# A list scheduler in the kernel for ScalarE's and VectorE's order in the FFNs, and two transposed blocks to a PSUM bank

## The chip, the cores and the metric

The kernel runs on one core of a Trainium2 chip. Its time is the device time of one execution in microseconds; the time before is the median of three runs, 957.65 us (956.59 to 960.48). The engines that matter are TensorE (PE in the profile; PEld is its weight load), VectorE (DVE), ScalarE (ACT), GpSimd (POOL), and SyncE (SP), which only starts DMAs here.

## What is computed

A trunk of two layers over 256 tokens of width 1024, in float32. Each layer is a half-step SwiGLU FFN, a mixer of a pooling group and a gated recurrence, and a second FFN, each followed by a layer norm. The change concerns the FFNs, four in all, with an inner width of 2816:

```python
D_MODEL, SEQ, DEPTH = 1024, 256, 2
D_FF = ((8 * D_MODEL // 3 + 127) // 128) * 128

def swiglu(x, w_gate, w_up, w_down):
    return (jax.nn.silu(x @ w_gate) * (x @ w_up)) @ w_down

for l in range(DEPTH):
    x = layer_norm(ALPHA * x + 0.5 * swiglu(x, ffn1_gate[l], ffn1_up[l], ffn1_down[l]), ln_g[l, 0], ln_b[l, 0])
    ...
    x = layer_norm(ALPHA * x + mix, ln_g[l, 1], ln_b[l, 1])
    x = layer_norm(ALPHA * x + 0.5 * swiglu(x, ffn2_gate[l], ffn2_up[l], ffn2_down[l]), ln_g[l, 2], ln_b[l, 2])
```

## The kernel before

**Numbers.** Every float32 operand is split into a high half in float32r and the remainder (`halves`, L114: ScalarE casts, VectorE subtracts). A product is three matmuls, high by high, high by low, low by high (`mm3`, L109 to 112). A weight arrives as a raw tile of 128 x 1024 (512 KB) by a DMA on SP's queue (L142) into one of five raw slots; ScalarE casts it to `wh` (gate and up weights) or `dh` (down weights) at L115, VectorE makes `wl` or `dl` at L116. Eight such pairs are held for gate and up, six for down.

**Groups.** The inner width is cut into eleven groups g of 256. `G` (one half of the tokens, hf) and `GT` (both halves, result transposed) compute a group's gate and up; `D` multiplies the gated group by its down weights into PSUM accumulators (`acc`). A `GT` has 32 matmuls of 128 x 512 with the high weights (`gu<-xt,wh`, the high pass) and 32 of 128 x 256 with the low ones (`gu<-xt,wl`, the low pass), all at L536. It holds all four PSUM banks of the pool `psg` (tiles named `gu`). Its result comes out with the inner dimension on the partitions, as D wants it; ScalarE and VectorE copy, add, gate and halve it (`gate_turned`, L553 to 563).

**Pairs.** In the three FFNs that are not the first, the groups 4 and 5, and 7 and 8, are computed as two pairs by a scheme of seven products instead of eight. Step `A` has 36 matmuls, step `B` 48; VectorE makes the sums of raw weights that they need (L225, L230 to 233). After B, ScalarE copies one accumulator (`u`, L491), VectorE makes four sums of 128 x 512 (L492 to 495), and then three times a silu (ScalarE, L505) and a product (VectorE, L506) give blocks of gated values in tiles named `cb`: u, p5 and v; a fourth, c11, was already made after A. These have the tokens on the partitions, so each of the four must be transposed for D: `T` (L648 to 657) does two transposes of 128 x 128 at L651 into a PSUM bank of its own, ScalarE casts the high half `hth`, VectorE subtracts `htl`, and the bank is free again.

**Order.** TensorE's order is the order of the code. Each FFN's steps stand in a list (`order`, L384 to 409); behind a pair come D of the two halves of the group before the pair and then GT of the group after it. Work that waits for another engine, such as T, is put into a queue, `Later` (L47 to 73), with a number of slots; a slot passes with each `mm3`, or with its length in GT. The slots of a pair's four T are 2, 6, 7 and 7 (L498 to 500). GT first empties that queue (`later.wait(lambda: not self.pending)`), since it needs all four banks. The order on ScalarE and VectorE is made by the tile scheduler when the program is built; the code steers it with priorities (AHEAD for gates, sums, products and halves of transposes, BEHIND for weight loads). Each engine then runs its instructions in that fixed order.

## Time and profile before

| what | us |
|---|---|
| median of three runs (lowest, highest) | 957.65 (956.59, 960.48) |
| the profiled execution | 958.14 |
| its span | 956.4 |
| TensorE, a `mm3` matmul of 128 x 512, mean | 0.39 |
| VectorE, a weight's low half of 128 x 1024 (`wl`, 255 of them), mean | 1.22 |
| ScalarE, a weight's high half (`wh`, 255 of them), mean | 1.05 |
| VectorE, 128 x 256 product or sum | 0.42 |
| DMA of a gate and up weight, issue to landing, median | 4.5 |

The durations of rows overlap: matmuls start 0.23 us apart though each is shown with 0.39, and VectorE's instructions also start before the one before them has ended. Where it matters, the text counts from start to start. The granted clock of TensorE is 0.998 of the full one in the profiled execution. In the rows of the timeline, a bracket at the end gives the idle time before the instruction and what ended it.

### The profile page before, as it was taken

The page shows a single profiled execution, that of the slowest core. Times are in us where ns is not written, and L with a number is a line of the kernel's source. Part 1 is how long each engine was busy: PE and PEld are TensorE (multiplying, and loading weights), DVE is VectorE, ACT ScalarE, POOL GpSimd, SP SyncE. Part 2 cuts the span into 40 slices and gives each one's busy share as a digit, 9 for nine tenths or more (in the row PEclk, how much of TensorE's full clock was granted, in tenths as well). Part 3 has the DMA queues.
Part 4 walks back from the last instruction along what each step waited for, and adds up shares of the span by engine and source line. Part 5 has one row for each costly group of instructions (what it writes and reads, how often), then busy time and mean ns, then how long its engine had stood idle before and what let it go on. Part 6 is the DMA issues. An engine that isn't in the chain of part 4 may idle for free.

```text
span 956.4 us, 13068 instructions
## 1 busy us (share of the span) xinstructions
PE 931.6 (97%) x4695; PEld 782.9 (82%) x4695; DVE 770.5 (81%) x1233; ACT 553.0 (58%) x840; POOL 22.7 (2%) x38
## 2 busy tenths in 40 slices
PE   9999999999999999989999989999999999999996
PEld 7888888888988887868888868788898888878685
DVE  6885755779879889897877799967899797899945
ACT  7775544377546656575455466753975466565630
POOL 0000000000010000000000000000000000000000
PEclk9999999999999999999999999999999999999999
DMA  8887853333725758878337578783417357588811
GB/s 301 314 297 265 286 205 112 141 116 105 243 89 192 277 180 285 276 273 287 122 135 261 169 251 295 271 290 100 136 63 264 130 187 260 190 277 280 271 78 45
DMA packets 57665, 198.92 MB, mean 208 GB/s; under 512 B 6784, under 2 KB 7040, under 8 KB 57600
## 3 DMA queue, kind: packets, MB, share of 16 engines
q1 hardware_dynamic: 57264, 197.43, 60.0%
q8 instruction: 37, 0.61, 0.3%
q0 software_dynamic: 192, 0.53, 0.2%
q14 instruction: 28, 0.23, 0.1%
q10 hardware_dynamic: 144, 0.13, 0.0%
HBM read 197.01 MB, written 1.05 MB: 207 GB/s over the span
## 4 chain that ended last, share of the span: by engine, by line
PE 76%; DVE 10%; DMA 9%; issue 3%; ACT 2%; SPq 0%; DVEq 0%; ACTq 0%
PE gu L111 24%; PE acc L111 22%; PE gu L536 22%; DMA raw<-in_gu 5%; DMA raw<-in_dn 3%; DVE wl L116 3%; PE gu L1006 2%; DVE dl L116 2%; PE acc L932 1%; PE gu L194 1%; PE acc L611 1%; ACT wh L115 1%; DVE htl L116 1%; PE acc L878 1%; ACT dh L115 1%
## 5 line engine op out<-in xcount | busy, mean ns | idle before, releaser
L115 ACT CAST wh<-raw 128x1024 fp32r<-128x1024 f32 x255 | 266.8, 1054 | 169.4 <-DMA raw<-in_gu 51.0
L116 DVE TENSOR_TENSOR wl<-raw,wh 128x1024 fp32r<-128x1024 f32 x255 | 306.6, 1220 | 28.0 <-ACT wh L115 25.3
L111 PE MATMUL gu<-wh,xt 128*128 128x512 f32 x720 | 239.2, 393 | 0.0
L111 PEld LDWEIGHTS gu<-wh,xt 128*128 128x128 f32 x720 | 135.1, 188 | 28.2 <-DVE xt L116 0.5
L536 PE MATMUL gu<-xt,wh 128*128 128x512 f32 x600 | 143.0, 392 | 3.6 <-DVE htl L116 2.9
L111 PE MATMUL gu<-wl,xt 128*128 128x512 f32 x360 | 140.5, 390 | 0.0
L111 PE MATMUL acc<-dh,hth 128*128 128x512 f32 x354 | 140.4, 397 | 0.0
L111 PE MATMUL acc<-dh,htl 128*128 128x512 f32 x354 | 138.1, 390 | 0.0
L111 PE MATMUL acc<-dl,hth 128*128 128x512 f32 x354 | 137.6, 389 | 0.0
L536 PEld LDWEIGHTS gu<-xt,wh 128*128 128x128 f32 x600 | 112.1, 188 | 31.1 <-DVE htl L116 7.2
L116 DVE TENSOR_TENSOR dl<-raw,dh 128x1024 fp32r<-128x1024 f32 x88 | 106.2, 1219 | 23.5 <-ACT dh L115 23.1
L115 ACT CAST dh<-raw 128x1024 fp32r<-128x1024 f32 x88 | 91.8, 1050 | 40.4 <-DMA raw<-in_dn 34.3
L111 PEld LDWEIGHTS gu<-wl,xt 128*128 128x128 f32 x360 | 67.7, 188 | 13.6
L111 PEld LDWEIGHTS acc<-dh,htl 128*128 128x128 f32 x354 | 66.4, 188 | 14.1
L111 PEld LDWEIGHTS acc<-dl,hth 128*128 128x128 f32 x354 | 66.6, 188 | 12.2
L111 PEld LDWEIGHTS acc<-dh,hth 128*128 128x128 f32 x354 | 66.6, 188 | 11.9
L536 PEld LDWEIGHTS gu<-xt,wl 128*128 128x128 f32 x600 | 74.8, 192 | 1.4
L536 PE MATMUL gu<-xt,wl 128*128 128x256 f32 x600 | 75.7, 283 | 0.0
L559 DVE TENSOR_TENSOR sil<-gu,sil 128x256 f32<-128x256 f32 x42 | 17.6, 419 | 40.4 <-ACT sil L558 40.3
L111 PE MATMUL gu<-wl,Sh 128*128 128x512 f32 x96 | 37.7, 392 | 0.8 <-DVE wl L116 0.8
L111 PE MATMUL gu<-wh,Sh 128*128 128x512 f32 x96 | 37.5, 391 | 0.0
L111 PE MATMUL gu<-wh,Sl 128*128 128x512 f32 x96 | 37.4, 390 | 0.0
(211 smaller groups left out, 1110.0 us busy)
## 6 DMA issues: line engine op xcount, KB each, us to landing
raw<-in_gu SPq DMA_DIRECT2D x208, 512.0 KB, 4.5
raw<-in_dn SPq DMA_DIRECT2D x88, 512.0 KB, 5.3
raw<-in_win SPq DMA_DIRECT2D x40, 512.0 KB, 4.4
raw<-in_wout SPq DMA_DIRECT2D x16, 512.0 KB, 4.5
lng<-in_ln_g SPq DMA_DIRECT2D x6, 512.0 KB, 6.4
lnb<-in_ln_b SPq DMA_DIRECT2D x6, 512.0 KB, 7.2
x<-in_first SPq DMA_DIRECT2D x4, 384.0 KB, 4.3
raw<-in_first SPq DMA_DIRECT2D x4, 384.0 KB, 6.3
```

The source lines that it names most:

```text
L111: nc.tensor.matmul(ps, a, b, start=start and n == 0, stop=stop and n == 2, skip_group_check=more)
L115: first = nc.scalar.copy(dst_h, src)
L116: return first, nc.vector.tensor_tensor(dst_l, src, dst_h.bitcast(F32), ALU.subtract)
L194: nc.tensor.transpose(pt[:, k - a, :], self.nat[:, k * P:(k + 1) * P], ident)
L536: nc.tensor.matmul(ps[i][part][:, 2 * S - w:], weight.parts[lo][:, c:c + P], x[:, 0:w], start=kt == 0 and not lo, stop=kt == KT - 1 and lo ...
L559: nc.vector.tensor_tensor(dst, p[:, 0:S], dst, ALU.add)
L611: nc.tensor.matmul(ps[i][part][:, 2 * S - w:], ws[k // 2].parts[lo][:, c:c + P], xs[:, 0:w], start=k == 0 and not lo, stop=k == KT - 1 and ...
L878: nc.tensor.matmul(pe[:, a:], lf[hf][c][:, h * P:(h + 1) * P], cumM[:, c, a:], start=True, stop=True)
L932: nc.tensor.matmul(dst[:, 2 * j:2 * j + 2, :], side[:, j, :], E[:, 2 * j:2 * j + 2, t0:t0 + dst.shape[2]], start=True, stop=True)
L1006: nc.tensor.matmul(ps[i // 2][:, i % 2, :], w, x, start=kt == 0 and n == 0 and i % 2 == 0, stop=kt == KT - 1 and n == 2 and i % 2 == 1)
```

## The change

Inside the FFNs, the order on ScalarE and VectorE is no longer made by the tile scheduler. Code in the kernel keeps a list of outstanding instructions (`Work`), each with a cost (a fixed part and a part for each column), what it must come after, and a rank; `Desk` holds a model time for each engine, advances with each matmul that is emitted, and emits the instruction that can start earliest by that model, lowest rank first. Weight casts and subtractions have ranks in the order of the weights; gates, sums, products and halves have rank 0. Each emitted instruction is pinned behind the one before it on its engine, without a semaphore. DMA starts follow a model of five raw slots with 1.65 us between loads and 4.6 us to land.

A pair's four blocks are transposed in two groups of two blocks, each group of four transposes into one PSUM bank; a group is emitted only when the model says that its products are done and a bank is free. GT behind a pair does its high pass block by block, 16 matmuls into the first two banks and then 16 into the other two, and asks for the last two only then. It no longer empties the whole queue first. No instruction is added or removed on any engine.

```diff
+LAG = 2
+FIXED, EACH = {"A": 0.155, "V": 0.153, "P": 0.95}, {"A": 0.000875, "V": 0.001042, "P": 0.0}
+HOP, DRAIN, LOAD, ARRIVE = 0.1, 0.25, 1.65, 4.6
+NORM, SUMS, GRACE = 6.5, 8, 0.25
+MM, MMN, FLIP = 0.2275, 0.1195, 0.11
...
 class Later:
...
     def run(self, until):
+        while True:
+            items = [q for q in self.queue if q[0] <= until and (q[3] is None or q[3]())]
+            if not items:
                 return
+            self.take(items)
...
+class Work:
...
+        self.cost = FIXED[engine] + width * EACH[engine]
...
+    def begin(self):
+        return max([self.at] + [a.done + HOP * (a.engine != self.engine) for a in self.after])
...
+class Desk:
...
+    def step(self, until=None):
+        best = None
+        for e in FIXED:
+            ready = [w for w in self.waiting if w.engine == e and w.ready()]
+            if not ready:
+                continue
+            at = max(self.free[e], min(w.begin() for w in ready))
+            w = min((w for w in ready if w.begin() <= at + GRACE * (w.rank < 1)), key=lambda w: w.rank)
+            at = max(at, w.begin())
+            if best is None or at < best[0]:
+                best = at, w
+        if best is None or until is not None and best[0] > until:
+            return False
+        at, w = best
+        self.waiting.remove(w)
+        ins = w.fn()
+        if w.engine != "P":
+            if w.engine in self.last:
+                self.pin(ins.ins, self.last[w.engine])
+            self.last[w.engine] = ins.ins.name
+        self.clock = w.done = self.free[w.engine] = at + w.cost
...
+    order = lambda ins, name: tc.add_manual_dep(
+        ins, name, mybir.DependencyInfo(mybir.DependencyClass.NoSync, mybir.DependencyReason.DATA), reason="in turn")
+    desk = Desk(order)
...
         def B(self, g):
-            later.wait(lambda: not self.pending)
...
-            for slots, n, hf, c in ((2, g, rows[0], self.c11), (6, g + 1, rows[0], u), (7, g + 1, rows[1], self.p5),
-                                    (7, g, rows[1], v)):
-                self.turn(slots, n, hf, c[:, GW:])
...
+            parts = [(g, rows[0], *self.c11), (g + 1, rows[0], u, self.product(u, two)),
+                     (g + 1, rows[1], p5, self.product(p5, three)), (g, rows[1], v, self.product(v, four))]
+            for some in (parts[:2], parts[2:]):
+                self.turn(LAG, *[(n, hf, c[:, GW:], work) for n, hf, c, work in some])
...
+        def turn(self, slots, *parts):
+            self.pending.update(part[:2] for part in parts)
+            later(slots, lambda: self.T(*parts), lambda: desk.over(*[part[3] for part in parts]) and Bank.free())
...
         def GT(self, g):
-            later.wait(lambda: not self.pending)
-            ps = [[psg.tile([P, 2 * S], F32, name="gu") for _ in range(2)] for _ in range(2)]
+            later.wait(lambda: self.turned(g - 1) or g - 1 in self.twice or all((g - 1, hf) in self.ht for hf in range(2)))
+            banks = [[Bank(), Bank()], None]
...
-                blocks = [[0], [1]] if lo or g == 2 and not self.first else [[0, 1]]
+                blocks = [[0], [1]] if lo or self.split(g) else [[0, 1]]
...
+        def split(self, g):
+            return not self.first and (g == 2 or g - 1 in self.twice)
...
+        def T(self, *parts):
+            desk.need(*[part[3] for part in parts])
+            bank, works = Bank(), []
+            for n, (g, hf, hn, _) in enumerate(parts):
+                pt = bank.tile[:, n * 2 * P:(n + 1) * 2 * P].rearrange("p (k t) -> p k t", k=2)
+                src = hn() if callable(hn) else hn
+                for i in range(2):
+                    nc.tensor.transpose(pt[:, i, :], src[:, i * P:(i + 1) * P], ident)
+                    desk.spend(FLIP)
+                works += self.turn_out(g, hf, pt)
+            bank.read(*works)
```

Tile names and lines of the changed kernel: `mm3` is at L234, a weight's halves at L303 and L306, the sums of raw weights at L454, GT at L807, T's transposes at L946 and its halves at L956 and L960, the copy of u at L758, the sums behind B at L756, silu and product at L772 and L773.

**TensorE** behind the first pair of the FFN that follows Mixer 0, from the 18th matmul of D behind B on. Before, T of c11 stands after the sixth matmul of D, u's after the 18th, and p5's and v's after the 21st of 24:

```order
L111 MATMUL acc<-dh,htl 128x512
L651 MATMUL gu<-ident,cb 128x128 x2
L111 MATMUL acc<-dh,hth 128x512
L111 MATMUL acc<-dl,hth 128x512
L111 MATMUL acc<-dh,htl 128x512
L651 MATMUL gu<-ident,cb 128x128 x4
L111 MATMUL acc<-dh,hth 128x512
L111 MATMUL acc<-dl,hth 128x512
L111 MATMUL acc<-dh,htl 128x512
L536 MATMUL gu<-xt,wh 128x512 x32
L536 MATMUL gu<-xt,wl 128x256 x32
```

After, from the 23rd matmul of D behind B on:

```order
L234 MATMUL acc<-dl,hth 128x512
L234 MATMUL acc<-dh,htl 128x512
L946 MATMUL gu<-ident,cb 128x128 x4
L807 MATMUL gu<-xt,wh 128x512 x3
L946 MATMUL gu<-ident,cb 128x128 x4
L807 MATMUL gu<-xt,wh 128x512 x29
L807 MATMUL gu<-xt,wl 128x256 x32
```

All 24 matmuls of D now come ahead of the first transposes; the second group stands behind three matmuls of GT. The same holds at all six pairs. In the FFNs behind the mixers, except the last, the transposes of group 10's first half also come three D matmuls later.

**VectorE** at the end of the same step B; L492 to L495 are the four sums, L506 the products, `htl` the transposes' low halves. Before:

```order
L116 TENSOR_TENSOR dl<-raw,dh 128x1024
L116 TENSOR_TENSOR wl<-raw,wh 128x1024 x4
L492 TENSOR_TENSOR cb<-cb,gu 128x512
L116 TENSOR_TENSOR wl<-raw,wh 128x1024
L493 TENSOR_TENSOR cb<-cb,gu 128x512
L494 TENSOR_TENSOR cb<-cb 128x512
L116 TENSOR_TENSOR htl<-gu,hth 128x256
L495 TENSOR_TENSOR cb<-cb,gu 128x512
L506 TENSOR_TENSOR cb<-cb 128x256 x2
L116 TENSOR_TENSOR dl<-raw,dh 128x1024
L506 TENSOR_TENSOR cb<-cb 128x256
L116 TENSOR_TENSOR htl<-gu,hth 128x256
```

After, from the last sum of raw weights on:

```order
L454 TENSOR_TENSOR raw<-raw 128x512
L306 TENSOR_TENSOR dl<-raw,dh 128x1024 x2
L306 TENSOR_TENSOR wl<-raw,wh 128x1024 x4
L756 TENSOR_TENSOR cb<-cb,gu 128x512 x2
L756 TENSOR_TENSOR cb<-cb 128x512
L756 TENSOR_TENSOR cb<-cb,gu 128x512
L773 TENSOR_TENSOR cb<-cb 128x256 x3
L306 TENSOR_TENSOR wl<-raw,wh 128x1024
L960 TENSOR_TENSOR htl<-gu,hth 128x256 x4
```

The four sums and three products stand together, behind two `dl` and four `wl`, and the four `htl` follow in one piece. Before, a `wl`, an `htl` and a `dl` stood among them.

**ScalarE** at the same place; L491 is the copy of u, L505 a silu, `hth` the transposes' high halves. Before:

```order
L115 CAST wh<-raw 128x1024 x4
L491 COPY cb<-gu 128x512
L115 CAST wh<-raw 128x1024
L115 CAST dh<-raw 128x1024
L115 CAST hth<-gu 128x256
L115 CAST dh<-raw 128x1024
L505 ACTIVATE cb<-cb 128x256 x2
L115 CAST dh<-raw 128x1024
L505 ACTIVATE cb<-cb 128x256
L115 CAST hth<-gu 128x256
L115 CAST dh<-raw 128x1024
L115 CAST hth<-gu 128x256 x2
```

After, L758 is the copy, L772 the silu:

```order
L303 CAST wh<-raw 128x1024 x4
L758 COPY cb<-gu 128x512
L303 CAST wh<-raw 128x1024
L303 CAST dh<-raw 128x1024
L772 ACTIVATE cb<-cb 128x256 x3
L303 CAST dh<-raw 128x1024
L956 CAST hth<-gu 128x256 x4
L303 CAST dh<-raw 128x1024 x2
```

The three silu stand together behind one `wh` and one `dh`, where the first two stood behind a `wh`, two `dh` and an `hth`, and the third behind one `dh` more. The four `hth` follow with one `dh` between.

On SP the order of the DMAs differs only in the loads of the norm's two rows, one group of weights earlier in three FFNs; on POOL one `pow` stands earlier at the end of the first FFN.

## Prediction

> **What bounds the kernel now.** I read the page first, then busy time by stretches, then what TensorE waits for, then its timeline behind the pairs.

> ```profile
> span 956.4 us, 13068 instructions
> PE 931.6 (97%) x4695; PEld 782.9 (82%) x4695; DVE 770.5 (81%) x1233; ACT 553.0 (58%) x840; POOL 22.7 (2%) x38
> ```

> TensorE (PE) is busy 97% of the span, VectorE (DVE) 81%, ScalarE (ACT) 58%. So the end is set by TensorE's own work, 931.6 us, plus the 24.8 us in which it stands still. The change adds no work to TensorE and takes none away. It can only win in those 24.8 us (more by start times, below).

> The stretches show where they lie. The columns are length, then PE, PEld, DVE, ACT and POOL with counts, the granted clock, DMA share and GB/s. The first is in the first FFN, which has no pairs; the six others run from the end of each pair's step B to the start of the low pass of the GT behind it.

> ```profile
> 8.70:165.00 156.30, 156.29 (x835) 135.43 (x836) 109.82 (x161) 98.23 (x158) 0.00 (x0) 1.00 0.73 255
> 369.12:385.81 16.69, 14.47 (x65) 11.08 (x64) 15.23 (x21) 10.35 (x16) 0.00 (x0) 1.00 0.83 283
> 419.68:437.32 17.64, 15.10 (x65) 10.92 (x64) 15.98 (x21) 12.54 (x18) 0.00 (x0) 1.00 0.83 294
> 558.16:575.51 17.35, 14.40 (x66) 11.08 (x64) 15.20 (x21) 10.35 (x16) 0.00 (x0) 1.00 0.77 276
> 609.38:625.93 16.55, 14.89 (x66) 10.99 (x64) 15.50 (x21) 11.30 (x18) 0.00 (x0) 1.00 0.79 270
> 843.20:859.68 16.48, 14.48 (x65) 11.08 (x64) 15.19 (x21) 10.61 (x18) 0.00 (x0) 1.00 0.80 273
> 893.55:910.99 17.44, 15.13 (x65) 10.93 (x64) 15.96 (x21) 12.04 (x18) 0.00 (x0) 1.00 0.80 277
> ```

> The first FFN has nothing to win: 156.29 of 156.30 us. The six stretches behind the pairs last 102.15 us together (16.69 + 17.64 + 17.35 + 16.55 + 16.48 + 17.44), each with the same work. The view of waits names the causes (total us, times, longest):

> ```profile
> PE gu L651 <- DVE cb L506: 8.9, 9, 2.3
> PE gu L536 <- DVE htl L116: 2.9, 3, 1.0
> PE gu L111 <- DVE wl L116: 0.8, 1, 0.8
> ```

> L651 is a transpose T, waiting for VectorE's product (L506). L536 is GT, waiting for the subtraction that gives a transpose's PSUM bank back. Both stand only in the six stretches; the 0.8 us at L111 is a weight's low half in a step B.

> **The change, term by term.** First the price of a stretch without stalls: 24 D matmuls, GT's high pass of 32 matmuls, eight transposes.

> ```profile
> 791.09 11.11 PE gu L536 x64
> 802.20 5.46 PE acc L111 x24
> 17.19 7.46 PE L536 MATMUL gu<-xt,wh 128*128 128x512 f32 x32
> 24.49 1.72 PE L536 MATMUL gu<-xt,wl 128*128 128x256 f32 x13
> 471.70 1.04 PE L194 MATMUL gu<-ident,x 128*128 128x128 f32 x8
> 472.49 0.48 PE L111 MATMUL acc<-dh,hth 128*128 128x512 f32 x1
> 472.81 0.40 PE L111 MATMUL acc<-dl,hth 128*128 128x512 f32 x1
> ```

> The 24 D take 5.46 us (0.2275 each); the high pass takes 24.49 - 17.19 = 7.30 us; eight transposes take 472.49 - 471.70 = 0.79 us, and the next matmul starts 0.32 instead of 0.23 us after the one before it, so 0.88 in all. Together 13.64 us, six times 81.8. The ceiling of the gain is 102.15 - 81.8 = 20.3 us. The first pair of the FFN behind Mixer 0 shows how the excess is made up:

> ```profile
> 373.23 0.39 PE L111 MATMUL acc<-dh,htl 128*128 128x512 f32 x1
> 375.18 0.44 PE L651 MATMUL gu<-ident,cb 128*128 128x128 f32 x2 [1.56 <-DVE cb L506]
> ...
> 377.07 0.41 PE L651 MATMUL gu<-ident,cb 128*128 128x128 f32 x2 [0.53 <-DVE cb L506]
> ...
> 378.02 7.96 PE L536 MATMUL gu<-xt,wh 128*128 128x512 f32 x32
> 385.81 3.99 PE L536 MATMUL gu<-xt,wl 128*128 128x256 f32 x32
> ```

> Start to start, u's transposes come 375.18 - 373.23 - 0.23 = 1.72 us late, v's by at least the 0.53 of its row, and the high pass takes 7.79 instead of 7.30 because its third and fourth bank come back late. The second pair of each FFN pays the last kind as a whole wait:

> ```profile
> 428.31 1.00 PE L536 MATMUL gu<-xt,wh 128*128 128x512 f32 x2
> 430.28 7.21 PE L536 MATMUL gu<-xt,wh 128*128 128x512 f32 x30 [0.97 <-DVE htl L116]
> ```

> 430.28 - 428.31 for two matmuls of 0.23 is 1.5 us of standing still. What a stretch keeps is at least the 13.64 us above; if the switches to and from the transposes make these twice as dear, 14.52. I take 14.0, nearer to the lower end because D and GT run without loss in the rows of the chain. **18.1 us** go: 102.15 less six times 14.0 (ends: 20.3 and 15.0).

> Now what the change does there. The transposes move behind all 24 D, as two groups of four: the first (c11 and u) is due 24 matmuls or 5.46 us after B's end, where c11 was due after 6 and u after 18; the second (p5 and v) after four transposes of 0.11 and three matmuls of GT more, 5.46 + 0.44 + 0.68 = 6.6 us. Both must find VectorE's products done. Its four sums and three products now stand together behind four `wl`, with no `wl`, `dl` or `htl` between, which is the second half of the gain. I place them for this pair with its own rows, in which a row of three gives VectorE's start spacing.

> ```profile
> 365.20 3.50 DVE L116 TENSOR_TENSOR wl<-raw,wh 128x1024 fp32r<-128x1024 f32 x3
> 369.07 1.22 DVE L116 TENSOR_TENSOR wl<-raw,wh 128x1024 fp32r<-128x1024 f32 x1 [0.37 <-ACT wh L115]
> 372.45 0.68 DVE L493 TENSOR_TENSOR cb<-cb,gu 128x512 f32<-128x512 f32 x1
> 373.04 0.68 DVE L494 TENSOR_TENSOR cb<-cb 128x512 f32<-128x512 f32 x1
> 376.51 0.42 DVE L506 TENSOR_TENSOR cb<-cb 128x256 f32<-128x256 f32 x1
> 370.22 1.05 ACT L115 CAST wh<-raw 128x1024 fp32r<-128x1024 f32 x1 [0.70 <-DMA raw<-in_gu]
> 372.01 1.05 ACT L115 CAST dh<-raw 128x1024 fp32r<-128x1024 f32 x1 [0.74 <-DMA raw<-in_dn]
> 374.25 0.71 ACT L505 ACTIVATE cb<-cb 128x256 f32<-128x256 f32 x2
> ```

> The fourth `wl` is over at 370.3. Four sums 0.6 apart (373.04 - 372.45) end by 372.8. ScalarE's three silu stand behind one `wh` and one `dh` cast, which waits for its DMA until 372.01 and ends at 373.06; at 0.35 each they run to 374.1. With 0.42 for a product, u is over at 373.8 and v at 374.5, not at 376.93 as before. Needed: 369.12 + 5.46 = 374.6 and 375.7. So both groups find their operands, 0.8 and 1.2 us ahead. In the second pairs VectorE is further ahead of TensorE (row 414.55 below), and the lead should be larger. The four `hth` and `htl` follow at once, and GT's second pair of banks is asked for 13 matmuls (3.0 us) after the second group, some 1.5 us after the last `htl`. The stall is gone unless one of these leads is.

> What comes late next is the last `wl` of step B in the second pair, since TensorE gets there three microseconds earlier and VectorE has hardly any idle time between the pairs:

> ```profile
> 376.93:417.18 40.25, 39.98 (x190) 33.31 (x191) 37.34 (x49) 23.24 (x32) 0.00 (x0) 1.00 0.79 262
> 414.55 2.35 DVE L116 TENSOR_TENSOR wl<-raw,wh 128x1024 fp32r<-128x1024 f32 x2
> 417.18 0.39 PE L111 MATMUL gu<-wl,Sh 128*128 128x512 f32 x1
> ```

> The first of these two `wl` ends at 415.8 and is used at 417.18, a lead of 1.4 us. TensorE comes 16.69 - 13.64 = 3.05 us earlier here, and 3.71 and 2.84 in the two other FFNs. If VectorE's stream stayed where it is and the lead is 1.4 in all three, 3.05 + 3.71 + 2.84 - 4.2 = 5.4 us would be given back; if it moves forward with the products, by 376.93 - 374.5 = 2.4 us, nothing here and little there. I take **1.0**, nearer to nothing because the products move and the 40.25 - 37.34 = 2.9 us of idle time give way.

> [...]

> **Small terms.** The transposes of G10's first half come behind nine D instead of six in two FFNs, so their halves are three matmuls (0.7 us) later for D10: zero to 0.7 each, I take 0.25. The subtractions of the transposed activations at the start of the three pair FFNs stand behind one `dl` more: zero to 0.5 each, a tenth taken. Together 0.6. The 0.8 us wait at L111 is left in. ScalarE's and VectorE's instruction counts are the same, the DMA order on SP differs by two loads of the norm's rows one group earlier, and POOL's pow in the first FFN is hidden in 156 us without a wait.

> **Sum** against the profiled execution, 958.14 us (a span of 956.4 and 1.74 around it): 958.14 - 18.1 + 1.0 + 0.6 = 941.6. That execution lies 0.5 above the median of the runs shown, 957.65, so I forecast **941.0 us**.

> **The rivals.**
> *VectorE becomes the bound between the pairs.* For it: 37.34 of 40.25 us busy. Against: the products come forward. All 5.4 given back in place of 1.0 is 945; with half as much again at the weights of A and GT, which the same stream makes, 948.

> *Only the place on TensorE helps, the products stay as late as now.* u's transposes now start at 375.18, 0.6 us after the first group is due, and v's product ends at 376.93, 1.2 after the second. Some 1.2 us in each first pair, half in each second one, where one wait fewer stands: 3.6 + 1.8 = 5.4, so 946 to 947.

> *The pin doesn't bring what its table says, or every microsecond moves to the next weight wait.* Then the time stays at 955 to 959. For it: DMA is at 0.77 to 0.83 in these stretches. Against: no wait of TensorE for a weight is in the list but 0.8 us.

> *Slower.* ScalarE runs in a fixed order, so the three silu now stand behind a `dh` cast whose DMA was already late (0.74 us of waiting in the row above).

> ```profile
> raw<-in_dn SPq DMA_DIRECT2D x88, 512.0 KB, 5.3
> ```

> If that load lands L later, TensorE stands at the first transpose for L - 0.8, with nothing else to run. It decides from L = 3.8 (0.8 + 18.1/6); with a whole landing of 5.3 us the six pairs cost 27 us, and the time is 958.1 - 18.1 + 27 - 0.5 = 966. Against: the loads keep their order and come from the same slots. [...]

> **How the numbers follow.** Forecast (937 to 945) 0.68; VectorE bound 0.10; products late 0.10; no change 0.06; slower 0.06. The floor is 958.1 less 20.3, less the 0.8 at L111, less 0.5: 936.5, which I round to 937, as the whole ceiling is unlikely. The upper end takes in both middle rivals with 2 us of room. A measurement of this kernel tells about 0.5% (4.8 us) from no change; the three first cases lie beyond it, less a remainder: faster 0.87, same 0.07, slower 0.06.

> **What would show it.** In the changed profile the waits for `cb` should fall from 8.9 us to under 1.5, those for `htl` from 2.9 to under 0.5, and each of the six stretches should last 13.7 to 14.3 us. VectorE's busy time should stay at 770 us within 2, its share rising as the span shrinks. A new wait for `wl` in the second step B, above 1 us, would show the first rival; transposes that still wait for `cb` the second; a silu long after its sum, behind a `dh` cast, the fourth. The forecast is wrong if the loads land later than now, since every lead worked out here is about one microsecond.

## The result, and the profile after

| | before | after |
|---|---|---|
| median of the runs, us (lowest, highest) | 957.12 (955.40, 960.48) | 983.40 (982.28, 984.08) |
| ratio to before, 95% interval | | 1.0269 [1.0239, 1.0299] |
| the profiled execution, us | 958.14 | 983.54 |
| its span, us | 956.4 | 981.8 |
| granted TensorE clock | 0.998 | 0.978 |
| six stretches from B's end to GT's low pass, us | 102.15 | 82.0 |
| six steps B (48 matmuls each), us | 67.1 | 99.4 |
| first FFN, GT1's start to the D after GT2, us | 27.70 | 41.30 |

The change makes the kernel 2.7% slower where 1.7% faster was forecast. The three last rows of the table hold nearly all of it: -20.1 + 32.3 + 13.6 = +25.8 us, against +25.4 in the span. The page of the changed kernel (busy time, then two rows of its 40 slices in tenths):

```profile
span 981.8 us, 13056 instructions
PE 942.6 (96%) x4695; PEld 792.5 (81%) x4695; DVE 777.5 (79%) x1233; ACT 552.3 (56%) x840; POOL 22.0 (2%) x38
...
PE   9599999999999999989999999899999999999896
...
PEclk9799999999999999989999999999999999999898
```

TensorE has the same 4695 matmuls and is busy 11 us longer: some of them ran slower (48 start 0.43 us apart in place of 0.23). The second slice is a hole, and the granted clock dips there and again near the pairs. The forecast's gain is there all the same. These are the six stretches from the end of a pair's step B to the start of GT's low pass in the changed kernel, with the columns of the prediction:

```profile
386.19:399.90 13.71, 13.71 (x65) 11.35 (x64) 12.07 (x18) 8.72 (x15) 0.00 (x0) 1.00 0.63 221
441.04:454.68 13.64, 13.64 (x66) 11.29 (x64) 10.71 (x16) 8.04 (x14) 0.00 (x0) 1.00 0.54 191
578.47:592.14 13.67, 13.67 (x66) 11.29 (x65) 11.58 (x18) 8.61 (x14) 0.00 (x0) 1.00 0.64 215
632.72:646.38 13.66, 13.66 (x66) 11.29 (x64) 11.96 (x18) 8.83 (x14) 0.00 (x0) 1.00 0.58 207
868.27:881.91 13.64, 13.64 (x65) 11.29 (x64) 11.86 (x18) 8.23 (x13) 0.00 (x0) 1.00 0.59 205
922.72:936.41 13.69, 13.69 (x66) 11.29 (x65) 11.54 (x18) 8.50 (x14) 0.00 (x0) 1.00 0.62 197
```

They sum to 82.0 us, at the floor of 81.8. What TensorE waits for now is elsewhere. Its view of waits (total us, times, longest) in the changed kernel has no row for a transpose and none for `htl`:

```profile
PE gu L807 <- DVE sil L836: 11.2, 2, 10.3
PE gu L234 <- DVE wl L306: 10.2, 9, 1.8
PE gu L234 <- ACT wh L303: 8.2, 6, 2.0
```

The first row is GT2 in the first FFN, waiting for the gates of GT1. The two others are weights' halves in the six steps B. The steps B as windows, first of the changed kernel, then two of before:

```profile
370.90:386.19 15.29, 13.01 (x49) 10.02 (x48) 13.76 (x15) 9.55 (x11) 0.00 (x0) 0.89 0.75 260
422.86:441.04 18.18, 14.41 (x49) 10.55 (x48) 17.48 (x20) 11.15 (x12) 0.00 (x0) 0.81 0.79 274
563.32:578.47 15.15, 12.86 (x50) 9.99 (x49) 14.26 (x15) 9.71 (x12) 0.00 (x0) 0.89 0.81 262
615.09:632.72 17.63, 13.60 (x50) 9.99 (x49) 16.23 (x18) 10.61 (x12) 0.00 (x0) 0.90 0.80 267
852.91:868.27 15.36, 13.07 (x50) 10.07 (x48) 14.07 (x15) 9.58 (x11) 0.00 (x0) 0.89 0.78 262
904.87:922.72 17.85, 14.10 (x50) 10.29 (x48) 16.65 (x18) 10.91 (x12) 0.00 (x0) 0.81 0.78 267
```

```profile
408.77:419.68 10.91, 10.91 (x49) 9.01 (x48) 9.66 (x11) 7.61 (x8) 0.00 (x0) 1.00 0.77 259
545.86:558.16 12.30, 11.53 (x50) 8.93 (x49) 10.31 (x12) 7.06 (x8) 0.00 (x0) 1.00 0.75 237
```

Before, five of six lasted 10.9 to 11.2 us, and 545.86 was the one that waited for a `wl`. Now all six are long, the second pair's more than the first's. VectorE is not the limit: it idles in four of the rows for over a microsecond, and the weights still come late.

**Where the first FFN stops.** GT1's low pass is over at 27.4 us; ScalarE copies its accumulators (L838) and VectorE adds to the copies (L836), which frees the banks for GT2. Before, the first copy ran at 26.54, still inside the low pass:

```profile
26.54 0.37 ACT L558 COPY sil<-gu 128x256 f32<-128x256 f32 x1 [2.17 <-PE gu L536]
```

ScalarE's timeline in the changed kernel:

```profile
38.46 1.04 ACT L303 CAST dh<-raw 128x1024 fp32r<-128x1024 f32 x1 [1.79 <-DMA raw<-in_dn]
40.62 1.04 ACT L303 CAST dh<-raw 128x1024 fp32r<-128x1024 f32 x1 [1.12 <-DMA raw<-in_dn]
41.58 0.37 ACT L838 COPY sil<-gu 128x256 f32<-128x256 f32 x1
```

Two `dh` casts stand pinned ahead of the copies and wait for their DMAs, the last until 40.62. Six casts of earlier loads (at L243, 27.91 to 36.67) also run ahead of the copies here. The copy itself waits for nothing. TensorE, meanwhile:

```profile
43.32 1.22 PE L807 MATMUL gu<-xt,xh 128*128 128x512 f32 x2 [10.29 <-DVE sil L836]
```

The table put the casts there by its own clock: its model of loads starts empty when the first FFN opens, though 15 loads have been issued by then. In its clock these two land 6.25 and 7.9 us after the opening and GT1's gates come at 9.44 (numbers that the list scheduler gives while the kernel is built); on the chip the loads land 22 and 24 us after it.

**What is late in step B.** ScalarE (ACT) and VectorE (DVE) ahead of the first pair's step A, changed kernel; step A starts at 359.95:

```profile
355.43 0.37 ACT L838 COPY sil<-gu 128x256 f32<-128x256 f32 x1 [6.79 <-PE gu L807]
355.84 0.42 DVE L836 TENSOR_TENSOR sil<-gu,sil 128x256 f32<-128x256 f32 x1 [4.55 <-ACT sil L838]
361.88 2.14 DVE L454 TENSOR_TENSOR raw<-raw 128x512 f32<-128x512 f32 x3
```

The same place before, where step A starts at 347.01:

```profile
336.53 0.69 DVE L230 TENSOR_TENSOR raw<-raw 128x512 f32<-128x512 f32 x1 [0.17 <-DMA raw<-in_gu]
...
342.49 0.37 ACT L558 COPY sil<-gu 128x256 f32<-128x256 f32 x1 [0.75 <-PE gu L536]
```

Before, the sums of raw weights for step B begin 10.5 us ahead of step A, ahead of GT's gates (L558). Now ScalarE stands 6.79 us and VectorE 4.55 us with nothing to do, because the pinned order has GT's gates next; the sums of step B's first weights (L454) come behind all of the gates, 1.9 us after step A has started. By the trace their loads had landed 9.0, 7.7 and 5.3 us ahead of step A. By the table's clock they land 0.4 to 3.7 us behind its start, so it saw no reason to put the sums in front. B's first `wl` ends 5.20 us after A's start (2.04 before), its last 22.03 (19.42). A raw slot comes free with its `wl`, so the next loads start later too: the first load of a `dh` behind these starts 12.7 us after A's start (9.7 before).

### The profile page after: what moved, and what is told of

Read it like the earlier page. It is cut to its first block, busy times and chain, and to the rows that moved or that the text cites. A ratio compares the mean times of both kernels' runs of the same rounds, so it can differ in the third digit from the quotient of the medians.

```text
span 981.8 us, 13056 instructions
## 1 busy us (share of the span) xinstructions
PE 942.6 (96%) x4695; PEld 792.5 (81%) x4695; DVE 777.5 (79%) x1233; ACT 552.3 (56%) x840; POOL 22.0 (2%) x38
## 3 DMA queue, kind: packets, MB, share of 16 engines
HBM read 197.01 MB, written 1.05 MB: 202 GB/s over the span
## 5 line engine op out<-in xcount | busy, mean ns | idle before, releaser
L303 ACT CAST wh<-raw 128x1024 fp32r<-128x1024 f32 x191 | 197.4, 1050 | 107.9 <-DVE raw L454 35.4
L306 DVE TENSOR_TENSOR wl<-raw,wh 128x1024 fp32r<-128x1024 f32 x191 | 229.1, 1221 | 30.4 <-ACT wh L303 30.0
L234 PE MATMUL gu<-wh,xt 128*128 128x512 f32 x720 | 240.4, 394 | 0.0
L234 PEld LDWEIGHTS gu<-wh,xt 128*128 128x128 f32 x720 | 136.0, 189 | 29.0 <-DVE xt L248 0.9
L807 PE MATMUL gu<-xt,wh 128*128 128x512 f32 x600 | 142.0, 392 | 0.0
L234 PE MATMUL gu<-wl,xt 128*128 128x512 f32 x360 | 141.0, 392 | 0.0
L234 PE MATMUL acc<-dh,hth 128*128 128x512 f32 x354 | 138.9, 393 | 0.0
L234 PE MATMUL acc<-dh,htl 128*128 128x512 f32 x354 | 138.1, 390 | 0.0
L234 PE MATMUL acc<-dl,hth 128*128 128x512 f32 x354 | 137.6, 389 | 0.0
L807 PEld LDWEIGHTS gu<-xt,wh 128*128 128x128 f32 x600 | 111.7, 188 | 23.0
L306 DVE TENSOR_TENSOR dl<-raw,dh 128x1024 fp32r<-128x1024 f32 x80 | 94.8, 1220 | 16.9 <-ACT dh L303 16.5
L303 ACT CAST dh<-raw 128x1024 fp32r<-128x1024 f32 x80 | 83.1, 1052 | 34.2 <-DMA raw<-in_dn 32.2
L243 ACT CAST wh<-raw 128x1024 fp32r<-128x1024 f32 x64 | 67.3, 1058 | 22.8 <-PE acc L234 8.0
L234 PEld LDWEIGHTS gu<-wl,xt 128*128 128x128 f32 x360 | 68.2, 189 | 13.9
L234 PEld LDWEIGHTS acc<-dh,htl 128*128 128x128 f32 x354 | 66.5, 188 | 14.4 <-DVE htl L960 0.3
L234 PEld LDWEIGHTS acc<-dh,hth 128*128 128x128 f32 x354 | 66.8, 189 | 13.0 <-ACT hth L956 0.4
L234 PEld LDWEIGHTS acc<-dl,hth 128*128 128x128 f32 x354 | 66.6, 188 | 12.9
L807 PEld LDWEIGHTS gu<-xt,wl 128*128 128x128 f32 x600 | 74.8, 192 | 1.4
L807 PE MATMUL gu<-xt,wl 128*128 128x256 f32 x600 | 75.7, 283 | 0.0
L454 DVE TENSOR_TENSOR raw<-raw 128x512 f32<-128x512 f32 x96 | 63.9, 687 | 1.7 <-DMA raw<-in_gu 0.9
L836 DVE TENSOR_TENSOR sil<-gu,sil 128x256 f32<-128x256 f32 x42 | 17.7, 421 | 54.9 <-ACT sil L838 54.9
## 6 DMA issues: line engine op xcount, KB each, us to landing
raw<-in_gu SPq DMA_DIRECT2D x208, 512.0 KB, 4.5
raw<-in_dn SPq DMA_DIRECT2D x88, 512.0 KB, 4.9
raw<-in_win SPq DMA_DIRECT2D x40, 512.0 KB, 4.3
raw<-in_wout SPq DMA_DIRECT2D x16, 512.0 KB, 4.4
lng<-in_ln_g SPq DMA_DIRECT2D x6, 512.0 KB, 6.8
lnb<-in_ln_b SPq DMA_DIRECT2D x6, 512.0 KB, 7.3
```

The lines of the kernel that those rows point to most:

```text
L234: nc.tensor.matmul(ps, a, b, start=start and n == 0, stop=stop and n == 2, skip_group_check=more)
L243: first = nc.scalar.copy(dst_h, src)
L303: return nc.scalar.copy(self.parts[0], self.raw)
L306: second = desk("V", ET, lambda: nc.vector.tensor_tensor(self.parts[1], self.raw, self.parts[0].bitcast(F32), ALU.subtract), [first], rank ...
L454: return desk("V", 512, lambda: nc.vector.tensor_tensor(dst, a, b, op), after, rank, None, **kw)
L807: nc.tensor.matmul(banks[i][part].tile[:, 2 * S - w:], weight.parts[lo][:, c:c + P], x[:, 0:w], start=kt == 0 and not lo, stop=kt == KT - ...
```

## The experiments

Two theories at the start. **The table's order**: both losses come from an order fixed by a model that has the loads late (step B) or early (first FFN). **The place**: TensorE reaches each step B three microseconds sooner, and weights would be late in any order. All sums below are counted from the starts of matmuls in the timeline of one profiled execution each (that of e1_backlog, 973.28 us, lies 4.2 over its median); the ratio is to the kernel before on the same chip.

| kernel | median us | ratio, 95% | six stretches | first B, three | second B, three | first FFN |
|---|---|---|---|---|---|---|
| before | 957.12 | 1 | 102.15 | 34.4 | 32.7 | 27.70 |
| after | 983.40 | 1.0269 [1.0239, 1.0299] | 82.0 | 45.8 | 53.7 | 41.30 |
| e1_backlog | 969.06 | 1.0125 [1.0108, 1.0142] | 83.0 | 46.7 | 54.8 | 27.70 |
| e5_nopin | 946.49 | 0.9890 [0.9875, 0.9905] | 89.5 | 33.0 | 34.6 | 27.68 |
| e6_pin_act | 982.82 | 1.0272 [1.0252, 1.0293] | 83.1 | 40.7 | 55.7 | 42.46 |
| e4_peonly | 988.17 | 1.0335 [1.0317, 1.0353] | 132.0 | 34.8 | 32.7 | 27.70 |
| e7_peonly2 | 969.12 | 1.0134 [1.0103, 1.0165] | 111.2 | 35.0 | 32.7 | 27.68 |
| e13_castbehind | 951.64 | 0.9936 [0.9913, 0.9958] | 97.4 | 32.7 | 33.0 | 27.68 |
| e9_pinwin | 945.01 | 0.9879 [0.9853, 0.9905] | 81.9 | 32.8 | 38.9 | 27.68 |
| e11_pinfew | 947.15 | 0.9893 [0.9874, 0.9912] | 92.4 | 32.7 | 32.7 | 27.68 |
| e10_grace0 | 957.83 | 1.0023 [1.0009, 1.0038] | 82.4 | 41.3 | 44.9 | 27.68 |
| e14_arrive | 979.61 | 1.0229 [1.0208, 1.0250] | 89.7 | 38.5 | 51.2 | 27.70 |
| **e12_pinwin_grace0** | **943.68** | **0.9855 [0.9835, 0.9875]** | 82.5 | 32.7 | 37.9 | 27.68 |
| e15_pinwin_arrive | 951.74 | 0.9947 [0.9931, 0.9963] | 83.7 | 32.7 | 41.5 | 27.68 |

**The load queue in the first FFN.** When the scheduler opens in the first FFN, its clock is told that the loads already issued need 17.5 us more.

```diff
 def open_desk(busy):
...
     desk.start(busy)
+    arrived[0] = desk.now + (17.5 if not busy else 0.0)
```

> The changed kernel with one number changed: at the opening of the scheduler's table in the first FFN, the model's load clock starts at 17.5 us instead of 0, so that the 15 loads issued before it count as still under way. In the changed kernel's trace TensorE stands at GT 2 of the first FFN for 10.3 and 0.9 us and then runs at half clock for some 2 us, while ScalarE's gate copy waits behind two dh casts whose loads land late. Theory A (the model's empty load queue puts these two casts ahead of the gates): that stop is gone, the first FFN is 13 to 14 us shorter, the rest is unchanged, time 969 to 971 us. Rival B (the loads or the ring of raw slots are what is late, whatever the order): the stop stays within 2 us, time 981 to 984.

969.06 us, and the first FFN is back at 27.70. The stop of 10.29 us is gone, and nothing else: the waits for weights in step B stand, 9.6 us for `wh` and 9.2 for `wl`.

So the empty queue in the table's clock costs some 14 us (983.40 - 969.06), 13.6 of them in this one window of the first FFN.

**No pin at all.** The table still sets the order in which the code emits, but the tile scheduler may reorder.

```diff
         if w.engine != "P":
-            if w.engine in self.last:
-                self.pin(ins.ins, self.last[w.engine])
             self.last[w.engine] = ins.ins.name
```

> The changed kernel without the pin: the same table emits the instructions in the same order, but nothing holds an instruction behind the one emitted before it, so the tile scheduler may put a weight's cast or a sum of raw weights ahead of gates that are not ready. Theory A (the fixed order makes weight casts and raw sums stand behind GT's gates while both engines are idle; step B then waits for wl and wh): step B falls from 15.1-15.4 and 17.6-18.2 us to 11-12.5 in all six, the first FFN loses its stop, the six stretches behind B stay near 13.7 to 14.5, time 937 to 946. Rival B (the weights are late because their loads are, since the loads are issued in the table's order, or because TensorE comes earlier): step B stays above 14 us, time 960 or more.

946.49 us. The first FFN is whole, the steps B are back at 33.0 and 34.6, and the stretches are 14.75 to 15.10 us, 89.5 together, a little more than expected. What TensorE still waits for in this kernel:

```profile
PE gu L805 <- DVE htl L958: 2.5, 3, 1.0
PE gu L944 <- DVE cb L771: 2.2, 3, 0.8
PE gu L232 <- DVE wl L304: 1.2, 2, 0.9
```

TensorE gets to the steps B nearly as early as in the changed kernel, and they aren't late by 32 us but by half a microsecond in all (67.6 against 67.1). The place as the cause falls; the fixed order is it. Without the pin 7.5 us of the stretches' gain are lost.

**Pinned on ScalarE alone.**

```diff
-            if w.engine in self.last:
+            if w.engine == "A" and w.engine in self.last:
```

> The changed kernel with the pin on ScalarE alone, VectorE free. If ScalarE's fixed order (casts behind the gates' copies) carries the loss, step B stays at 14 to 18 us and the stop in the first FFN stays, time 972 to 984. If VectorE's fixed order (sums of raw weights behind the gates' additions) carries it, step B falls to 11 to 13 us and only the first FFN's stop of 13 us is left, time 948 to 958.

982.82 us (two runs), as the changed kernel. In TensorE's waits the first FFN's stop is there unchanged, and ScalarE's `wh` come latest in the steps B, by up to 4.7 us:

```profile
PE gu L234 <- ACT wh L303: 14.4, 5, 4.7
PE gu L807 <- DVE sil L836: 11.6, 2, 10.7
```

ScalarE's fixed order is enough for the whole loss, but the steps B lose their time here in another way than in the changed kernel. VectorE is free, and it makes the sums as soon as their loads land, the first 9.3 us ahead of step A (361.58). What holds ScalarE up is two `dh` casts that wait for their DMA, pinned ahead of the `wh` for which TensorE then waits (first pair, VectorE ahead of step A, then ScalarE in step B):

```profile
352.25 0.69 DVE L454 TENSOR_TENSOR raw<-raw 128x512 f32<-128x512 f32 x1
...
377.62 1.05 ACT L303 CAST dh<-raw 128x1024 fp32r<-128x1024 f32 x1 [2.20 <-DMA raw<-in_dn]
380.26 1.05 ACT L303 CAST dh<-raw 128x1024 fp32r<-128x1024 f32 x1 [1.59 <-DMA raw<-in_dn]
```

In each of the six steps B such casts wait 2.8 to 6.1 us in all; in the changed kernel it is at most 0.9. How much VectorE's fixed order alone would do wasn't run.

**TensorE's part without the table.** The kernel before, with blocks two to a bank, both groups behind the 24 D, and GT's high pass in two halves; ScalarE and VectorE are left to the tile scheduler.

```diff
-            for slots, n, hf, c in ((2, g, rows[0], self.c11), (6, g + 1, rows[0], u), (7, g + 1, rows[1], self.p5),
-                                    (7, g, rows[1], v)):
-                self.turn(slots, n, hf, c[:, GW:])
+            self.turn(8, *parts[:2])
+            self.turn(9, *parts[2:])
...
-                blocks = [[0], [1]] if lo or g == 2 and not self.first else [[0, 1]]
+                blocks = [[0], [1]] if lo or not self.first and (g == 2 or g - 1 in twice) else [[0, 1]]
```

> The kernel before with only TensorE's part of the change: a pair's blocks transposed two to a bank behind all 24 matmuls of D, the second group three matmuls into GT, GT's high pass block by block; ScalarE's and VectorE's order stays with the tile scheduler and its priorities. Theory A (place and banks of the transposes remove most of the stall, the table of ScalarE's and VectorE's order is not needed for it and brings the loss): the six stretches last 13.7 to 14.8 us, step B 11 to 12.5, no stop in the first FFN, time 937 to 943. Rival B (the gain behind the pairs comes from the sums and products standing together by the table): transposes still wait for cb by 0.5 to 1.3 us in each pair, stretches 14.3 to 15.2, time 944 to 950. Rival C (with TensorE earlier by 3 us the weights of step B are late whatever the order): stretches 13.7 but step B 14 us or more, time 953 or more.

988.17 us. The time alone would suit rival C, but no step B is late, and stretches of 21 to 23 us were in no expectation. The timeline of TensorE in this kernel shows a wait of my own making: T's halves were emitted after each block, so the second block's transposes wait until VectorE has read the first block out of the same bank.

```profile
373.79 0.38 PE L659 MATMUL gu<-ident,cb 128*128 128x128 f32 x2
378.22 0.69 PE L659 MATMUL gu<-ident,cb 128*128 128x128 f32 x2 [4.05 <-DVE htl L116]
```

The run says nothing on the question; the next one mends it, with all four transposes of a bank ahead of the halves, as in the changed kernel.

```diff
+            blocks = [bank[:, n * 2 * P:(n + 1) * 2 * P].rearrange("p (k t) -> p k t", k=2) for n in range(len(parts))]
-            for n, (g, hf, hn) in enumerate(parts):
-                pt = bank[:, n * 2 * P:(n + 1) * 2 * P].rearrange("p (k t) -> p k t", k=2)
+            for pt, (g, hf, hn) in zip(blocks, parts):
                 for i in range(2):
                     nc.tensor.transpose(pt[:, i, :], hn[:, i * P:(i + 1) * P], ident)
+            for pt, (g, hf, hn) in zip(blocks, parts):
```

> As e4_peonly, but the four transposes of a group are emitted before the casts and subtractions that read their bank; in e4 those of the first block stood between, and in the trace the second block's transposes wait 3.8 to 4.8 us (first group) and 1.3 us (second) for the first block's htl in the same bank, 30 us in all. Theory A (place and banks alone remove most of the stall; the table isn't needed): the six stretches last 13.7 to 15, step B 11 to 12.5 us, time 938 to 946. Rival B (without the table's order the products come 0.5 to 1.3 us late in each pair): stretches 14.5 to 16, time 946 to 952. Rival C (step B's weights are late whatever the order because TensorE comes earlier): step B over 14 us, time over 953.

969.12 us. Again the time is rival C's without its sign: the steps B are as before (35.0 and 32.7), and the stretches are longer than before, which no expectation had. The transposes wait for products nearly as long as before (8.1 us, 8.9 before), and GT waits far longer for the `htl` that give its banks back:

```profile
PE gu L542 <- DVE htl L116: 11.2, 6, 3.1
```

Before, that was 2.9 us. VectorE in this kernel, behind the first pair:

```profile
375.02 0.68 DVE L495 TENSOR_TENSOR cb<-cb,gu 128x512 f32<-128x512 f32 x1
375.62 2.35 DVE L116 TENSOR_TENSOR dl<-raw,dh 128x1024 fp32r<-128x1024 f32 x2
377.89 0.41 DVE L507 TENSOR_TENSOR cb<-cb 128x256 f32<-128x256 f32 x1
```

Two `dl` stand between the last sum and v's product, and the second group of transposes waits 2.17 us for it. So the new place on TensorE gains nothing without the table's order behind the pair. The table's order without the new place wasn't run.

**The casts behind the gates, in the kernel before.** If late casts alone made step B late, this edit would.

```diff
                 first, second = halves(wh, wl, raw)
+                if copied[0] and self.ring == "w" and scope[0]:
+                    tc.add_manual_dep(first.ins, copied[0].ins.name,
+                                      mybir.DependencyInfo(mybir.DependencyClass.NoSync, mybir.DependencyReason.DATA),
+                                      reason="behind the gates")
...
-                    nc.scalar.copy(dst, p[:, S:2 * S])
+                    copied[0] = nc.scalar.copy(dst, p[:, S:2 * S])
```

> The kernel before with one rule of order more: in the FFNs each cast of a gate and up weight that is issued stands behind the last copy of a gate that was issued ahead of it on ScalarE. In the changed kernel the casts stand so, and ScalarE is idle for 6.8 us ahead of the gates of the GT before the first pair. Theory A (that place of the casts alone makes the weights of step B late): first steps B go from 10.9-12.3 to 13-15.5 us, second ones to 12-16, the six stretches stay at 16 to 19, time 966 to 980. Rival B (it takes VectorE's fixed order too, the sums of raw weights behind the gates): step B within 1 us of before, time 955 to 961.

951.64 us, faster than before by 0.6% and below both expectations, and no step B is late, though ScalarE stands longer ahead of the gates than in the changed kernel:

```profile
342.74 0.37 ACT L562 COPY sil<-gu 128x256 f32<-128x256 f32 x1 [9.56 <-PE gu L540]
```

Theory A falls. Here VectorE is free to make the sums of raw weights during ScalarE's idle time, and the casts follow among the gates and behind them. In the changed kernel the sums themselves come late. But e6_pin_act has its sums early too and loses nearly as much, so late sums aren't needed for the loss either: a whole pinned order on ScalarE can make it with the `dh` casts. How the 32.3 us of the changed kernel divide among late sums, late casts and late loads stays open.

**Pinned only behind the pairs.** The pin holds from the end of B to the end of the next GT's high pass, the place for which the forecast needed it.

```diff
-        if w.engine != "P":
+        if w.engine != "P" and self.tight:
...
+            desk.tight, desk.last = True, {}
...
+                if lo:
+                    desk.tight = False
```

> The changed kernel with the pin kept only from the end of each step B to the end of the high pass of the GT behind it (copy of u, sums, products, halves of the transposes and the weights among them); everywhere else the table's order is emitted but not pinned, as in e5_nopin, whose six stretches last 14.75 to 15.1 us (e5) against 13.64 to 13.71 (changed kernel). Theory A (the pin is worth some 1.2 us behind each pair and costs 4 to 7 us ahead of each step B and 13.5 in the first FFN): stretches 13.6 to 13.9, step B 10.9 to 12.1, time 938 to 941. Rival B (holding the order behind the pair delays the weights of the next step B): step B of the second pairs 13 us or more, time 946 to 952.

945.01 us, better than both kernels and between the two expectations. The stretches keep the gain (81.9), the first steps B and the first FFN are whole, and the second steps B keep 2 us each, rival B's sign: 13.12, 13.28 and 12.55. The next run pins in this window only the works of rank 0, not the weights:

```diff
-        if w.engine != "P" and self.tight:
+        if w.engine != "P" and self.tight and w.rank < 1:
```

> e9_pinwin, but in the window behind each step B only copies, sums, silu, products and the transposes' halves are pinned behind each other; weight casts and subtractions there are free. In e9 the second steps B last 13.1, 13.3 and 12.6 us, in e5 (no pin at all) 10.9, 12.1 and 11.6. Theory A (the products must be kept free of weights, so the pin has to hold the weights back too): with weights free the stretches go back to 14.8 to 15.5 us, the second steps B to 11 to 12, time 944 to 949. Rival B (the pin among the products is enough): stretches 13.6 to 14, second steps B 11 to 12, time 938 to 941.

947.15 us. Now the second steps B are whole as well (32.7), but the stretches are 14.35 to 16.77, because weights are let in between sums and products again. Both effects are one trade: holding weights back behind a pair wins some 10 us there and costs some 6 in the second steps B.

**The table's preference for gates.** GRACE lets a work of rank 0 be taken up to 0.25 us before it can start, over a weight that could start now. This is e1_backlog without it. The table's own clock has the first and the second step B 5.07 and 7.15 us over their matmuls' time with GRACE, and 5.0 and 4.4 without.

```diff
-NORM, SUMS, GRACE = 6.5, 8, 0.25
+NORM, SUMS, GRACE = 6.5, 8, 0.0
```

> e1_backlog with one number of the table more: GRACE 0 instead of 0.25, so that a weight that can start now no longer waits for a gate or product that may start within 0.25 us. Everything stays pinned. The table's own clock, which runs while the kernel is built, gives step B of the second pairs 7.15 us over its 48 matmuls of 0.2275 with GRACE 0.25 (the chip: 18.3 - 10.9 = 7.4 in e1) and 4.4 with 0; of the first pairs 5.1 and 5.0 (the chip: 4.3 to 5.4). Theory A (step B's wait is made by the order that the table pins, and its clock foresees it): second steps B last 15 to 16 us instead of 18.3, first ones 15 to 16 as in e1, time 958 to 963. Rival B (step B waits for loads that the table doesn't order): step B as in e1, time 967 to 972.

957.83 us, 11 less than e1_backlog and level with before within 0.5%; the second steps B fell from 54.8 to 44.9 (4.0 each over their 10.9), the first from 46.7 to 41.3. The table's clock had a loss in the steps B before any run. For the second ones it was right with GRACE 0 as well (4.4 against 4.0); for the first ones it saw no change, and they came down by 1.8 us each.

**The table's landing time of a load.** Back to e1_backlog, with 1.65 us for a load to land in place of 4.6.

```diff
-HOP, DRAIN, LOAD, ARRIVE = 0.1, 0.25, 1.65, 4.6
+HOP, DRAIN, LOAD, ARRIVE = 0.1, 0.25, 1.65, 1.65
```

> e1_backlog with one number of the table changed: a load is taken to land 1.65 us after its start in the table's clock instead of 4.6. Everything stays pinned; no load is started earlier by it. e13 has shown that casts behind the gates' copies alone do not make step B late. In the trace of the changed kernel the loads of step B's first three weights of the first pair land 9.0 to 5.3 us ahead of step A's start, and their first sum stands at 1.9 us after it, behind all of GT's gates; the table's clock has them land 0.4 to 3.7 us after step A's start. Theory A (the table takes loads for late that have landed, so their sums and casts are pinned behind the whole row of gates): earlier landings in the table move sums and casts forward, first steps B fall from 15.2-16.3 to 12-14 us, second ones from 18.3 to 14-16, time 948 to 960. Rival B (step B's weights are late because the pinned order as such is in the way, whatever landing it assumes; casts pinned ahead of gates then wait for their loads and hold the gates up): step B over 15 and 17 us, or waits for gates appear, time 965 to 980.

979.61 us. The first steps B fell, as expected, from 46.7 to 38.5; the second hardly, and a loss opened elsewhere, since a load that the table now believes too early is one that a pinned cast waits for. ScalarE, and TensorE's waits, in this kernel:

```profile
363.67 1.05 ACT L303 CAST dh<-raw 128x1024 fp32r<-128x1024 f32 x1 [3.90 <-DMA raw<-in_dn]
```

```profile
PE gu L947 <- DVE cb L774: 6.4, 5, 1.7
PE gu L947 <- DVE hn L859: 6.0, 2, 3.2
```

The four columns together are 5 us shorter than in e1_backlog, and the span is 7 us longer, so some 12 us are lost elsewhere; TensorE's wait for `hn` stands at group 10, behind the second pairs. This is the mechanism of the first FFN again, made on purpose. Too late a belief puts work behind what it could precede, too early a belief blocks the engine; one number doesn't fit both. Under a full pin the steps B take 34.4 us more than before in e1_backlog, 19.1 with GRACE 0 and 22.6 with the shorter landing time; both together under a full pin weren't run.

**The version that beats both.** The window of e9_pinwin, with GRACE 0:

```diff
-NORM, SUMS, GRACE = 6.5, 8, 0.25
+NORM, SUMS, GRACE = 6.5, 8, 0.0
...
-        if w.engine != "P":
+        if w.engine != "P" and self.tight:
```

> e9_pinwin with GRACE 0, which in e10 took the second steps B from 18.3 to 15.0 us under a full pin. Theory A (it lets weights pass gates that are about to start): second steps B 11 to 12.3 instead of 13.0 on average, stretches 13.6 to 14, time 939 to 943. Rival B (outside the pinned windows the tile scheduler has the say, so the number hardly counts): second steps B 12.5 to 13.3, time 943 to 946.

943.68 us, 1.45% under before and 4% under the changed kernel. Time and second steps B are as rival B had them: GRACE hardly counts outside the full pin, and the ratio's interval overlaps that of e9_pinwin. One stretch and one second step B in this kernel:

```profile
369.26:382.94 13.68, 13.68 (x66) 11.29 (x65) 12.84 (x18) 10.16 (x16) 0.00 (x0) 1.00 0.72 262
405.89:418.59 12.70, 11.47 (x49) 8.93 (x48) 11.92 (x13) 8.09 (x10) 0.00 (x0) 1.00 0.85 266
```

TensorE is busy for 927.3 of the span's 941.2 us, 99%. The second steps B still wait for three `wl`, 3.6 us together. The last run gives the same kernel the shorter landing time:

```diff
-HOP, DRAIN, LOAD, ARRIVE = 0.1, 0.25, 1.65, 4.6
+HOP, DRAIN, LOAD, ARRIVE = 0.1, 0.25, 1.65, 1.65
```

> e12_pinwin_grace0 (pin only behind step B, GRACE 0) with the same change of the landing time in the table. e12 has second steps B of 12.7, 12.6 and 12.6 us, 1.7 over their matmuls, and little else left. Theory A: the weights stand further forward in the pinned window as well, second steps B 11 to 12, stretches 13.6 to 14.2, time 937 to 942. Rival B (in the window the order of weights is what it is; casts ahead of the silu now wait for late dh loads): stretches 14.5 or more, time 944 to 952.

951.74 us: the second steps B rose to 41.5, and the stretches stay under the 14.5 of rival B. That lever is no help there, and why these steps keep their 1.7 us each stays open.

## Why the prediction was wrong

**The bound and the ceiling** were right. TensorE bounds the kernel, and the gain lay in the six stretches.

**18.1 us from the stretches** was right in mechanism and a little small: 102.15 - 82.0 = 20.1 us came, since a stretch keeps 13.67 us and not 14.0; the switches to and from the transposes cost nothing beyond the floor of 13.64. The signs named for it came: no wait for `cb`, none for `htl`, stretches of 13.6 to 13.7 (13.7 to 14.3 was named). It isn't owed to the late steps B, which give VectorE more time: in e9_pinwin, with short ones, the stretches keep 81.9.

**1.0 us at the last `wl` of step B in the second pair** is the step that failed. It measured 32.3 us, in all six steps B. The prediction took it "nearer to nothing because the products move and the 40.25 - 37.34 = 2.9 us of idle time give way", and its upper bound of 5.4 left VectorE's stream where it was. Both ends kept before's order ahead of the pair. But the table rules the order in the whole of each FFN, and ahead of step A it gave up the early sums and casts on which B lived; the idle time did not give way, it grew (4.55 us on VectorE and 6.79 on ScalarE in one piece ahead of the first pair; from the last product behind a first pair to the end of the second step B, VectorE idles 6.3, 7.6 and 7.0 us, before 3.9, 3.3 and 3.8). I had compared the orders behind the pairs alone. e5_nopin and e9_pinwin show that with another order ahead of the pairs the same place on TensorE costs 0.5 and 4.6 us (67.6 and 71.7, less 67.1), so the term was of the right kind for that change and off by the part that wasn't read.

**"The first FFN has nothing to win"** was true and not enough: it had 13.6 us to lose. Its order of casts was changed by the same table; in the order of ScalarE, two `dh` casts moved ahead of GT1's gate copies.

**The slower rival**, put at 966 us, had the right mechanism: ScalarE in fixed order, TensorE's next operand behind a `dh` cast that waits for its DMA. I looked for it at the three silu alone, where it does not occur. It stood at GT1's gates, with a price of 13.6 us once, in place of 27 us in six parts; in e6_pin_act it stands in the six steps B as well. Its 0.06 was too little for a risk that any place of any FFN could carry. **VectorE as the bound between the pairs** gave the sign that was named for it (a wait for `wl` above 1 us), but not its cause: VectorE idles ahead of the gates.

**VectorE's 770 us within 2** missed: 777.5. In e12_pinwin_grace0, with the same 1233 instructions, it is 770.7. Busy time counts an overlap once (in the kernel before, durations of 849.8 us in sum make 770.5 busy). The durations added up are nearly the same (852.1 and 849.8 us), and 347 of the instructions have idle time ahead of them, 268 before: most of the extra 7 us is overlap that is gone.

**Not in the sum at all** was the clock. In the changed kernel 48 matmuls of 512 columns start 0.43 us apart in place of 0.23, none in the kernel before: 48 x 0.20 = 9.6 us. They lie inside the 32.3 and 13.6 us, not on top of them. **The small terms** weren't told apart; the three sums of the result's table leave -0.4 us for them and all else.

## What to carry to other kernels

A table that pins an order rules everything between its first and its last instruction: compare the orders over that whole reach, and price each stop that it can make for the engine that sets the end, not only the place for which it was built. An engine in a pinned order that follows a model paid here for loads that the model had wrong, in either direction (13.6 us in the first FFN for loads believed too early, some 12 us in e14_arrive for the same, 8.2 us in the first steps B of e1_backlog for loads believed too late: 46.7 against 38.5); start such a model with the queue that exists, and pin only the stretch in which the order is needed (here 943.7 us in place of 983.4). Where the planner has a clock of its own, read its forecast first: it had the steps B 5 and 7 us over their time, and the chip showed 4.4 and 7.0. That it is so close is partly luck, since the chip's figures hold matmuls at half clock (0.43 us apart), which the planner doesn't have; with the shorter landing time it had 2.1 us for all six, and on the chip the second ones showed 6.2.

## What the runs showed of the hardware

In the changed kernel TensorE's granted clock fell from 1.00 to 0.50 not only in the stop of 10.29 us of the first FFN but also behind far shorter ones. Windows of 3.41 us, ahead of a drop and in it (the figure behind the count of POOL is the granted clock):

```profile
379.49:382.90 3.41, 1.38 (x5) 0.92 (x6) 3.41 (x4) 1.98 (x3) 0.00 (x0) 1.00 0.83 286
382.91:386.31 3.40, 3.40 (x10) 2.63 (x9) 1.91 (x3) 2.22 (x3) 0.00 (x0) 0.50 0.88 317
```

```profile
380.12 0.51 PE L234 MATMUL gu<-wh,Sh 128*128 128x512 f32 x1 [0.88 <-ACT wh L303]
382.03 0.51 PE L234 MATMUL gu<-wl,Sh 128*128 128x512 f32 x1 [1.40 <-DVE wl L306]
...
383.63 0.63 PE L234 MATMUL gu<-wh,Sh 128*128 128x512 f32 x1
384.06 0.63 PE L234 MATMUL gu<-wl,Sh 128*128 128x512 f32 x1
```

Two stops of 0.88 and 1.40 us leave 1.38 us of work in the first window. The clock falls at its end, 0.9 us after the second stop was over and with TensorE at work, and ten matmuls follow at 0.43 us. In the kernel before, a single stop of 2.27 us (row 564.89) did nothing; there it lies across two windows, if the grid is counted back from the change of the clock at that execution's end:

```profile
563.68:567.09 3.41, 1.66 (x10) 1.27 (x11) 3.22 (x7) 3.41 (x8) 0.00 (x0) 1.00 0.44 174
```
